# Order of the products inside a step: by part of the weights instead of by k tile

## Chip, cores, metric

The kernel runs on one core of one Trainium2 chip. The metric is device time in microseconds; of several runs the median is given. One more execution was taken with the hardware profiler, and all rows below are from it.

## What is computed

Two layers of a hybrid decoder trunk over 256 tokens of width 2048, all in float32. Each layer normalises its input, projects it with one wide matrix, feeds the columns of the result to four groups of heads (forgetting attention, differential attention, block-sparse attention, gated linear attention), gates each group and projects back:

```python
def reference(x, ...):
    for l in range(DEPTH):                      # DEPTH = 2
        h = rms_norm(x, norm_g[l])              # x: (1, 256, 2048)
        p = split_columns(h @ w_in[l])          # 7,700 columns
        mixed = concatenate([fox, diff, moba, gla])   # four gated head groups
        x = x + mixed @ w_out[l]
    return rms_norm(x, final_norm_g)
```

The large products are `h @ w_in` and `mixed @ w_out`. To keep float32 accuracy with TensorE's faster fp32r type, each operand is split into a high part and a low part, and three products stand for one: high x high, high x low, low x high.

## The kernel before

The weights of both projections are cut into **blocks** of 256 to 512 columns (`_blocks`, line 104), and each block into **steps** of 4 k tiles of 128 rows, or 2 where the block has 512 columns (`_steps`, line 142). The list `plan` holds all steps in the order in which they run. For each step one DMA on the SP queue brings its raw weights (`load`; 4 buffers), ScalarE rounds them to the high part (`hi_of`, line 387), VectorE subtracts to get the low part (`lo_of`, line 390), each into one of 4 buffers (`parts_of`, line 1221), and TensorE multiplies (`multiply`, line 1239). Loads run 4 steps and splits 3 steps ahead of the products.

There are two kinds of blocks that matter here. In a **rows** block the activations are the stationary operand and the weights move: the result has tokens on the partitions, two halves `m` of 128 tokens, each in its own PSUM bank. Per k tile and half there are three matmuls: activations high x weights high, high x low, low x high. All have the block's width: 512, 264 or 258 columns (256 in the last chunk of the output projection). In a **cols** block (256 columns of the weights) the weights are the stationary operand: the result has columns on the partitions, two groups `c` of 128, each in its own bank. Per k tile and group there are two matmuls: the high part with both planes of the activations (`hTp`, high beside low, 512 columns moving), and the low part with the high plane only (256 columns moving). Nine names of 512 columns are cols blocks, each in two halves, in both layers: 144 steps of 4 k tiles x 2 groups, so 8 pairs of matmuls each. A last block (`apart`) and the first step of the plan have orders of their own, which the change leaves alone.

The work of the head groups is written as Python generators (`tasks`). After each step of the plan `give_time` and `tick` let them issue some instructions, by a budget of costs; so small matmuls and transposes into "side" tiles stand on TensorE between steps, never inside one. All matmuls go through the helper `matmul` (line 283 in the rows of the profile), transposes through line 287, and VectorE and ScalarE instructions through line 187, so the profile shows those lines and tells instructions apart by tiles. In the profile a matmul's operands are written `out<-moving,stationary`: `mm<-hTp,hi` is the 512-column matmul of a cols step, `mm<-hTp,lo` the 256-column one; `mm<-hi,hTp`, `mm<-lo,hTp` and, in the output projection, `mm<-hi,mTh`, `mm<-lo,mTh`, `mm<-hi,mTl` are those of rows steps. Block 2 of the plan adds up in a side tile, so its 32 pairs appear as `side<-hTp,hi` and `side<-hTp,lo`.

Every matmul is issued with its own weight load (LDWEIGHTS, engine PEld in the profile).

Of the kernel before, what the change touches and what calls it, by code (L numbers as in the profile page):

```python
# [21 lines left out]
P = 128  # L22
SEQ = 256
# [193 lines left out]
def hybrid_trunk(  # L217
# [63 lines left out]
    def matmul(out, lhsT, rhs, start, stop, tiles=1):  # L281
        left["pe"] += int(np.prod(rhs.shape[1:])) * (4 if lhsT.dtype == F32 else 1) / 2400.0 / tiles
        t_.matmul(out, lhsT, rhs, start=start, stop=stop)  # L283
# [90 lines left out]
    hTp = big.tile([P, KT, 2, SEQ], F32R, name="hTp")  # L374
# [772 lines left out]
    for z in _steps():  # L1147
        b = blocks[z["block"]]
# [90 lines left out]
    def multiply(s):  # L1239
        b = s["block"]  # L1240
        n, (lh, ll) = b["n"], b["lhs"]
        if s["first"]:
            b["ps"] = side.get([P, 1024]) if b is blocks[2] else mm.tile([P, 1024], F32, name="mm")
        ps = b["ps"]
        if b["kind"] == "apart":
            b.setdefault("steps", []).append(s)
            if s["last"]:
                b["ps1"] = side.get([P, 1024])
            for m, o, steps in ((0, ps[:, :n], [s]), (1, b.get("ps1"), b["steps"])):
                if m == 1 and not s["last"]:  # L1250
                    break
                for z in steps:
                    for j, kt in enumerate(z["kts"]):
                        first, last = z["first"] and j == 0, z["last"] and j == len(z["kts"]) - 1
                        hi, lo, ts = z["hi"][:, j], z["lo"][:, j], slice(m * P, (m + 1) * P)
                        matmul(o[:, :n], lh[:, kt, ts], hi, first, False)
                        matmul(o[:, :n], lh[:, kt, ts], lo, False, False)
                        matmul(o[:, :n], ll[:, kt, ts], hi, False, last)
            return
        if s is plan[0]:  # L1260
            for js in ((0, 1), (2, 3)):
                for x, w in ((lh, s["hi"]), (ll, s["hi"]), (lh, s["lo"])):
                    for j in js:
                        for m in range(2):
                            matmul(ps[:, m * 512:m * 512 + n], x[:, j, m * P:(m + 1) * P], w[:, j],
                                   j == 0 and x is lh and w is s["hi"], False)
            return
        for j, kt in enumerate(s["kts"]):
            first, last = s["first"] and j == 0, s["last"] and j == len(s["kts"]) - 1
            hi, lo = s["hi"][:, j], s["lo"][:, j]  # L1270
            if b["kind"] == "rows":
                for m in range(2):
                    o, ts = ps[:, m * 512:m * 512 + n], slice(m * P, (m + 1) * P)
                    matmul(o, lh[:, kt, ts], hi, first, False)
                    matmul(o, lh[:, kt, ts], lo, False, False)
                    matmul(o, ll[:, kt, ts], hi, False, last)
            else:
                for c in range(2):
                    o, cs = ps[:, c * 512:(c + 1) * 512], slice(c * P, (c + 1) * P)
                    matmul(o, hi[:, cs], hTp[:, kt].rearrange("p z t -> p (z t)"), first, False)  # L1280
                    matmul(o[:, :SEQ], lo[:, cs], lh[:, kt], False, last)

    def results(b):
        ps, n = b["ps"], b["n"]
# [44 lines left out]
    for i, s in enumerate(plan):  # L1329
        if ("rb", 0) not in ready:  # L1330
            next(rms, None)
        prepare(i + ahead)
        if i in X_AT:
            c = slice(X_AT.index(i) * 512, X_AT.index(i) * 512 + 512)
            nc.sync.dma_start(xs[:, :, c], x[0, :, c].rearrange("(m p) c -> p m c", p=P))
        settle(waiting, s["first"] and len(waiting) > 1)
        while not s["need"] <= ready:
            tick(False)
        multiply(s)
        if s["last"] and s["block"]["done"]:  # L1340
            waiting.append(s["block"])
        give_time()
        tick()
    while tasks:
        tick(False)
    b = plan[-1]["block"]
# [29 lines left out]
```

## Time and profile before

| | us |
|---|---|
| median of 3 runs | 954.85 (954.78 to 955.5) |
| the profiled execution | 955.05 |
| its span, first to last instruction | 953.3 |
| TensorE matmuls busy | 940.7, 5,430 matmuls |
| TensorE weight loads busy | 819.4, 5,430 loads |
| VectorE busy | 616.8 |
| ScalarE busy | 480.9 |
| GpSimd busy | 68.5 |

The span is what the rows lie in; the profiled execution has 1.75 us more around it. A matmul's duration in the profile runs from its start to the modelled end of its passage through the array. The next one starts before that, so durations overlap and a sum of durations is more than the time they took. The distance between starts is what a matmul costs in a row of matmuls. "Busy" counts overlapping durations once.

### The profile page before, as it was taken

To read this page: it belongs to the slowest core of one execution; us is meant where nothing else is said; L and a number is where in the kernel's file an instruction comes from. 1 tells how busy PE (TensorE), PEld (TensorE's weight loads), DVE (VectorE), ACT (ScalarE), POOL (GpSimd) and SP (SyncE) were. 2 spreads that over 40 slices of the span, in tenths; PEclk is the share of its full clock that TensorE was granted. 3 is DMA by queue.
4 is the path that set the end of the run, shared out by engine and by line. 5 is a ranking of instruction groups with operands and counts; after the bars stand their busy time and mean duration, and the time that the engine had idled before them with its cause. 6 is when DMAs were issued, how large, how long until landed. Compare 5 with 4: busy or idle time off the path is not lost.

```text
span 953.3 us, 13796 instructions
## 1 busy us (share of the span) xinstructions
PE 940.7 (99%) x5430; PEld 819.4 (86%) x5430; DVE 616.8 (65%) x836; ACT 480.9 (50%) x653; POOL 68.5 (7%) x45
## 2 busy tenths in 40 slices
PE   9999999999999999999999999999999999999996
PEld 7989889888888888888898898898888888888886
DVE  7666776667756876555556668656675759755553
ACT  7675534454474446445446544445445644563451
POOL 0010200001110210000000102100011002100000
PEclk9999999999999999999999999999999999999999
DMA  8766565556655465556665544554555645655652
GB/s 312 223 198 204 181 189 157 155 157 195 178 187 178 140 210 163 167 181 180 195 174 161 159 156 155 171 173 156 175 178 177 197 161 177 228 167 165 196 179 89
DMA packets 49075, 170.19 MB, mean 179 GB/s; under 512 B 5969, under 2 KB 6513, under 8 KB 49010
## 3 DMA queue, kind: packets, MB, share of 16 engines
q1 hardware_dynamic: 46592, 165.24, 55.0%
q10 hardware_dynamic: 1778, 1.97, 0.7%
q0 software_dynamic: 640, 2.10, 0.7%
q8 instruction: 42, 0.69, 0.3%
q14 instruction: 23, 0.19, 0.1%
HBM read 167.19 MB, written 2.10 MB: 178 GB/s over the span
## 4 chain that ended last, share of the span: by engine, by line
PE 96%; issue 1%; DVE 1%; ACT 1%; DMA 1%; SPq 0%; POOLq 0%; POOL 0%; DVEq 0%; ACTq 0%
PE mm L283 86%; PE side L283 8%; PE side L287 2%; DMA raw<-in_weights 1%; ACT hi L187 1%; DVE mTl L187 0%; DVE xs L187 0%; DVE lo L187 0%; ACT gate L187 0%; SPq L1158 0%; POOLq L1372 0%; POOL rf L385 0%; ACT two L187 0%; SPq L1171 0%; DVE an L187 0%
## 5 line engine op out<-in xcount | busy, mean ns | idle before, releaser
L187 DVE TENSOR_TENSOR lo<-raw,hi 128x1024 fp32r<-128x1024 f32 (+3 forms) x301 | 380.7, 1269 | 299.7 <-ACT hi L187 296.3
L187 ACT ACTIVATE hi<-raw 128x1024 fp32r<-128x1024 f32 (+3 forms) x301 | 318.1, 1059 | 433.2 <-PE mm L283 390.1
L283 PE MATMUL mm<-hTp,hi 128*128 128x512 f32 x1120 | 397.6, 399 | 0.4 <-ACT gate L187 0.2
L283 PE MATMUL mm<-hTp,lo 128*128 128x256 f32 x1120 | 313.0, 279 | 0.8 <-DVE lo L187 0.8
L283 PE MATMUL mm<-hi,hTp 128*128 128x512 f32 (+2 forms) x1024 | 258.8, 339 | 0.0
L283 PEld LDWEIGHTS mm<-hTp,hi 128*128 128x128 f32 x1120 | 210.3, 188 | 50.2 <-ACT gate L187 0.4
L283 PEld LDWEIGHTS mm<-hTp,lo 128*128 128x128 f32 x1120 | 211.2, 189 | 1.2 <-DVE lo L187 1.1
L283 PEld LDWEIGHTS mm<-hi,hTp 128*128 128x128 f32 x1024 | 176.8, 189 | 21.7 <-ACT hi L187 0.5
L283 PE MATMUL mm<-lo,hTp 128*128 128x512 f32 (+2 forms) x512 | 171.2, 336 | 0.0
L283 PEld LDWEIGHTS mm<-lo,hTp 128*128 128x128 f32 x512 | 96.1, 189 | 9.6
L283 PE MATMUL mm<-hi,mTl 128*128 128x512 f32 (+1 forms) x256 | 96.5, 377 | 0.8 <-DVE mTl L187 0.8
L283 PE MATMUL mm<-hi,mTh 128*128 128x512 f32 (+1 forms) x256 | 96.8, 378 | 0.0
L283 PE MATMUL mm<-lo,mTh 128*128 128x512 f32 (+1 forms) x256 | 96.2, 376 | 0.0
L283 PEld LDWEIGHTS mm<-hi,mTl 128*128 128x128 f32 x256 | 48.2, 188 | 10.4 <-DVE mTl L187 1.7
L283 PEld LDWEIGHTS mm<-lo,mTh 128*128 128x128 f32 x256 | 48.2, 188 | 8.5
L283 PEld LDWEIGHTS mm<-hi,mTh 128*128 128x128 f32 x256 | 48.2, 188 | 8.5
L283 PE MATMUL side<-four,four 128*128 128x128 f32 (+2 forms) x288 | 38.0, 288 | 0.0
L919 POOL TENSOR_TENSOR four<-four,two 128x1024 f32<-128x1024 f32 x8 | 20.8, 2606 | 225.0 <-DVE four L187 225.0
L187 ACT ACT_TABLE_LOAD x27 | 34.6, 1283 | 0.5
L283 PEld LDWEIGHTS side<-four,four 128*128 128x128 f32 (+1 forms) x288 | 31.2, 190 | 2.6 <-issue 0.7
L187 DVE TENSOR_TENSOR both<-mm,both 128x512 f32<-128x512 f32 x35 | 23.9, 684 | 0.0
L187 ACT ACTIVATE four<-side,nb 128x256 f32<-128x256 f32 (+1 forms) x48 | 20.4, 434 | 0.1
(159 smaller groups left out, 618.2 us busy)
## 6 DMA issues: line engine op xcount, KB each, us to landing
raw<-in_weights SPq DMA_DIRECT2D x272, 512.0 KB, 3.7
raw<-in_weights SPq DMA_DIRECT2D x16, 516.0 KB, 3.7
raw<-in_weights SPq DMA_DIRECT2D x15, 528.0 KB, 4.4
xs<-in_x SPq DMA_DIRECT2D x4, 512.0 KB, 4.5
four<-in_xt SPq DMA_DIRECT2D x3, 512.0 KB, 7.1
out<-xs SPq DMA_DIRECT2D x6, 256.0 KB, 3.1
two<-in_const POOLq DMA_DIRECT2D x4, 256.0 KB, 3.6
two<-in_final_norm_g POOLq DMA_DIRECT2D x4, 256.0 KB, 5.6
```

The costliest lines, as they stand in the source:

```text
L187: return f(*args, **kw)
L283: t_.matmul(out, lhsT, rhs, start=start, stop=stop)
L287: t_.transpose(out, src, ident)
L919: g_.tensor_mul(sw, sw, over(f[:, 1], H))
```

## The change

Inside a step, all products with the weights' high part are issued first, then all with the low part. In a cols step that is eight 512-column matmuls and then eight 256-column ones, in place of eight alternating pairs. In a rows step it is high x high for all k tiles and halves, then low x high (both read the weights' high part), then high x low. The matmul that opens a bank's sum is still the first one there, and the one that closes it is now the last product with the low part. Steps, loads, splits, buffers and tasks are as before.

```diff
-        for j, kt in enumerate(s["kts"]):
-            first, last = s["first"] and j == 0, s["last"] and j == len(s["kts"]) - 1
-            hi, lo = s["hi"][:, j], s["lo"][:, j]
-            if b["kind"] == "rows":
-                for m in range(2):
-                    o, ts = ps[:, m * 512:m * 512 + n], slice(m * P, (m + 1) * P)
-                    matmul(o, lh[:, kt, ts], hi, first, False)
-                    matmul(o, lh[:, kt, ts], lo, False, False)
-                    matmul(o, ll[:, kt, ts], hi, False, last)
-            else:
+        order = list(enumerate(s["kts"]))
+        end = s["last"], len(order) - 1
+        if b["kind"] == "rows":
+            for x, part in ((lh, "hi"), (ll, "hi"), (lh, "lo")):
+                for j, kt in order:
+                    for m in range(2):
+                        matmul(ps[:, m * 512:m * 512 + n], x[:, kt, m * P:(m + 1) * P], s[part][:, j],
+                               s["first"] and j == 0 and x is lh and part == "hi", part == "lo" and (True, j) == end)
+            return
+        for part in ("hi", "lo"):
+            for j, kt in order:
                 for c in range(2):
-                    o, cs = ps[:, c * 512:(c + 1) * 512], slice(c * P, (c + 1) * P)
-                    matmul(o, hi[:, cs], hTp[:, kt].rearrange("p z t -> p (z t)"), first, False)
-                    matmul(o[:, :SEQ], lo[:, cs], lh[:, kt], False, last)
+                    o, w = ps[:, c * 512:(c + 1) * 512], s[part][:, j, c * P:(c + 1) * P]
+                    if part == "hi":
+                        matmul(o, w, hTp[:, kt].rearrange("p z t -> p (z t)"), s["first"] and j == 0, False)
+                    else:
+                        matmul(o[:, :SEQ], w, lh[:, kt], False, (True, j) == end)
```

## Rows read from the trace of the kernel before

**Rows 1.** The page: engines (busy, share, instructions), granted clock by slice, chain by engine.

```profile
PE 940.7 (99%) x5430; PEld 819.4 (86%) x5430; DVE 616.8 (65%) x836; ACT 480.9 (50%) x653; POOL 68.5 (7%) x45
...
PEclk9999999999999999999999999999999999999999
...
PE 96%; issue 1%; DVE 1%; ACT 1%; DMA 1%; SPq 0%; POOLq 0%; POOL 0%; DVEq 0%; ACTq 0%
```

**Rows 2.** Groups with shapes apart, whole span: count, busy us, mean ns, idle before.

```profile
L283 PE MATMUL mm<-hTp,hi 128*128 128x512 f32 x1120 | 397.6, 399 | 0.4 <-ACT gate L187 0.2 <-ACT hi L187 0.2
L283 PE MATMUL mm<-hTp,lo 128*128 128x256 f32 x1120 | 313.0, 279 | 0.8 <-DVE lo L187 0.8
...
L283 PE MATMUL mm<-hi,mTl 128*128 128x256 f32 x32 | 9.1, 283 | 0.0
```

**Rows 3.** Timeline, TensorE, 205 to 238 us: start us, duration us, what.

```profile
205.07 0.27 PE L283 MATMUL mm<-hTp,lo 128*128 128x256 f32 x1
...
238.00 0.28 PE L283 MATMUL mm<-hTp,lo 128*128 128x256 f32 x1
```

**Rows 4.** Timeline, TensorE, 326 to 352 us.

```profile
326.99 0.28 PE L283 MATMUL mm<-hTp,lo 128*128 128x256 f32 x1
...
352.08 0.28 PE L283 MATMUL mm<-hTp,lo 128*128 128x256 f32 x1
```

**Rows 5.** Groups with shapes apart, the stretch of rows 3.

```profile
L283 PE MATMUL mm<-hTp,hi 128*128 128x512 f32 x96 | 33.4, 394 | 0.0
L283 PE MATMUL mm<-hTp,lo 128*128 128x256 f32 x96 | 26.6, 277 | 0.0
```

**Rows 6.** Groups with shapes apart, the stretch of rows 4.

```profile
L283 PE MATMUL mm<-hTp,hi 128*128 128x512 f32 x72 | 25.6, 400 | 0.0
L283 PE MATMUL mm<-hTp,lo 128*128 128x256 f32 x72 | 20.2, 281 | 0.0
```

**Rows 7.** Timeline, TensorE, a rows run of 512 columns in the output projection.

```profile
866.08 0.39 PE L283 MATMUL mm<-lo,mTh 128*128 128x512 f32 x1
866.31 0.39 PE L283 MATMUL mm<-hi,mTl 128*128 128x512 f32 x1
866.53 0.39 PE L283 MATMUL mm<-hi,mTh 128*128 128x512 f32 x1
...
872.88 0.39 PE L283 MATMUL mm<-lo,mTh 128*128 128x512 f32 x1
```

**Rows 8.** Timeline, TensorE, where a run of 256 columns follows one of 512.

```profile
922.10 0.39 PE L283 MATMUL mm<-hi,mTl 128*128 128x512 f32 x1
922.33 0.28 PE L283 MATMUL mm<-hi,mTh 128*128 128x256 f32 x1
922.44 0.28 PE L283 MATMUL mm<-lo,mTh 128*128 128x256 f32 x1
922.56 0.28 PE L283 MATMUL mm<-hi,mTl 128*128 128x256 f32 x1
...
923.88 0.28 PE L283 MATMUL mm<-lo,mTh 128*128 128x256 f32 x1
```

**Rows 9.** Timeline, TensorE, where a rows run of 512 columns follows a cols step.

```profile
238.12 0.39 PE L283 MATMUL mm<-hi,hTp 128*128 128x512 f32 x1
...
239.96 0.61 PE L283 MATMUL mm<-hi,hTp 128*128 128x512 f32 x2
```

**Rows 10.** Timeline, TensorE, the first cols step (in brackets: idle before, released by).

```profile
9.53 0.50 PE L283 MATMUL mm<-hTp,hi 128*128 128x512 f32 x1 [0.16 <-ACT hi L187]
10.79 0.39 PE L283 MATMUL mm<-hTp,lo 128*128 128x256 f32 x1 [0.76 <-DVE lo L187]
11.01 0.39 PE L283 MATMUL mm<-hTp,hi 128*128 128x512 f32 x1
```

**Rows 11.** Timeline, the row sums on TensorE and the fold on VectorE before them.

```profile
30.50 0.95 PE L283 MATMUL side<-one,four 128*128 128x1 f32 x8
...
29.22 1.15 DVE L187 TENSOR_TENSOR four<-four 128x512 f32<-128x512 f32 x2
```

**Rows 12.** Waits of ScalarE: who for whom, us in total, times, longest.

```profile
ACT hi L187 <- PE mm L283: 390.1, 222, 6.0
```

## Prediction

> **What bounds the kernel now.** The page comes first, its table of engines and its chain [rows 1]. TensorE is busy for 99% of the span and the chain that ended last is TensorE for 96%, so only what TensorE does per matmul, or what it waits for, can move the time. The granted clock stands at the upper of its two levels, 2.4 GHz, in every slice; the change takes no matmul away, so I leave the clock as it is. Next I ask which matmuls fill the span: the groups of instructions with shapes kept apart [rows 2]. The "cols" blocks give 1,120 pairs of a 512-column matmul (hi) and a 256-column one (lo), and 32 pairs more go to a side tile: 1,152 pairs in 144 steps of 8. The "rows" blocks give runs in which all matmuls have one width. A matmul's duration in these rows is longer than the beat at which matmuls follow each other, because they overlap. So the beats are read from the timeline, as differences of starts.
>
> In one long cols stretch 95 pairs take 32.93 us, 346.6 ns a pair [rows 3]. In another 71 pairs take 25.09 us, 353.4 ns [rows 4]. It is the same code in the same order: the alternation of 512 and 256 has two beats, each held for a whole stretch. Which share has which? The mean duration of a lo matmul is 277 ns in the first stretch and 281 in the second [rows 5, 6], and 279 over the kernel [rows 2], so I take half and half: 350.0 ns a pair.
>
> The runs of one width are steadier. In a settled run of 512-column matmuls 30 of them take 6.80 us, 226.7 ns each [rows 7]; in a run of 256-column matmuls 11 take 1.32 us, 120.0 ns each [rows 8]. Both together are 346.7 ns, the shorter of the two beats.
>
> **The change, part by part.** *The cols steps.* Now: hi, lo, hi, lo. After: eight hi, then eight lo. Nothing is added or removed: as many matmuls, weight loads, bytes. If hi and lo in their groups run at the beats of the settled runs, a pair costs 346.7 ns in place of 350.0, 3.3 ns less. I count 1,104 pairs, the 1,152 less the 48 of the six steps before 30.5 us, which are dealt with below: 1,104 x 3.3 = 3.7 us less.
>
> Two corrections come from the edges of the groups. When a run of 512 follows a lo matmul, its first eight take 1.84 us [rows 9], where eight settled ones take 1.81: some 27 ns to settle. When 256 follows a settled 512 run, the first two take 0.23 us in place of 0.24 [rows 8], some 7 ns won. If each of the 138 steps paid the 27 ns, that would be 3.7 us; if none did, nothing. The settled phase may well carry over from the lo run to the next hi run, as it did from 512 to 256 in two matmuls, and then only steps behind other work of TensorE pay: the two long stretches hold 12 and 9 steps in a row (96 and 72 pairs [rows 5, 6]), so this is a minority, and I take a third, 1.2 us. The 7 ns on 138 steps are 0.9 us. Sum for the cols steps: 3.7 - 1.2 + 0.9 = 3.4 us less; ends 0.9 us less (every step pays) and 4.6 us less (none does). With a share of the long beat of 0.6 instead of a half the upper end is near 5.3.
>
> *The rows steps.* Now for each k tile and half of the rows three matmuls in a row go to one PSUM bank, and the first two have the same stationary tile; after, the bank changes with each matmul. All have one width. The rows show no price for either: from the last matmul of a bank to the first of the other it is 0.22 us, as anywhere in that run [rows 7], and the three of a group share its 0.68 us evenly, so that the one with a repeated stationary tile comes no sooner. I take nothing; TensorE's own back-to-back order covers it, since each weight load lies beside the matmul before it. Each nanosecond of error would be 1.5 us on the 1,536 matmuls of the input projection's rows blocks (16 k tiles x 2 halves x 3 products x 8 blocks x 2 layers), but I see no row that gives the error a sign.
>
> *The first wait.* At 9.53 us TensorE issues one hi matmul and then waits for the low part: its lo starts at 10.79 and the second pair at 11.01 [rows 10], so that the first pair takes 1.48 us where 0.35 would do, 1.13 too much. After the change seven more hi matmuls (1.6 us) lie before the first lo, and the wait goes. What is late next: at 30.50 us TensorE runs the row sums of the first norm, which need a fold on VectorE that ends at 30.37 [rows 11]. That fold hangs on loads of x and on ScalarE and VectorE, which at that time wait for loads and for each other, not for TensorE. So TensorE, come there 1.1 us sooner, would stand still until 30.4, and of the 1.13 us, and of all that the six cols steps before it win, 0.13 is left. Bounds: 0 and 1.1 us; I take 0.1.
>
> *What is moved past what.* Only TensorE's order changes; no DMA and no instruction of VectorE, ScalarE, SP or POOL changes place in its queue. The wait for the low part goes from the second matmul of a step to two thirds of it in rows (after both products with the high part) and to the middle of its matmuls in cols; behind it stand only the lo matmuls of that step. The high part's buffer comes free earlier, by a third of a step, and the low part's at the end as before. ScalarE stands waiting for such buffers for 390 us in 222 places [rows 12], so its next split starts earlier, but TensorE waits for splits only in the place above: worth nothing.
>
> **The sum.** 3.4 + 0.1 = 3.5 us less. The profiled execution is 955.05 us (span 953.3 and 1.75 around it), so 951.55; the median of the three runs is 0.2 lower than it, so the forecast is 951.4.
>
> **Row and rule.** The row: a settled 512 takes 226.7 ns and a settled 256 takes 120.0 [rows 7, 8], 13.3 ns above columns divided by 2.4 GHz, and a pair in alternation has a beat that is not always their sum. [...]
>
> **The rivals.** *(1) Every step pays the settling.* Each hi run is only eight long, as long as the settling, and before it a run of the other width. For it: [rows 9] and the long beat itself show that a change of width upsets the phase. Against it: the 512-to-256 change settles in two. Then the cols steps gain 3.7 - 3.7 + 0.9 = 0.9 us, with the start 1.0: 953.9.
>
> *(2) The order costs nothing.* A matmul's cost is a matter of its own width, and the two beats come from something else in a stretch (other engines' traffic in SBUF, say) that grouping leaves alone. For it: both beats occur in the same code. Against it: the runs of one width keep to one beat through all their stretches. Only the start is left: 954.8. [...]
>
> *(3) Slower: hi keeps its price and lo loses its discount.* In alternation lo is cheap: 279 ns of duration against 283 in a run of its own width [rows 2], so 116 ns of beat in place of 120, and hi takes the rest of the 350, 234. If hi is dear for what it reads (two planes of the activations as the moving operand, against one plane of weights in rows) and not for what stands beside it, then after the change a pair costs 234 + 120 = 354 ns, 4 more: 1,104 x 4 = 4.4 us more, less 0.1: 959.2. The place is every cols step, and it decides from a mean hi beat of 230 ns up. For it: no row shows these operands in a run of 512. Against it: at the short beat a pair with just these operands costs exactly the settled sum.
>
> **How the numbers follow.** A measurement of this kernel can tell about 0.2%, 1.9 us, from no change. Forecast 0.57, rival 1 0.25, rival 2 0.06, rival 3 0.12. The forecast lies beyond 1.9 us but for a small part of its ends: faster 0.56, same 0.32 (rivals 1 and 2 and that part), slower 0.12. The range reaches from the upper end of the gain (5.3 + 0.1: 949.5 against the median) to rival 2 with a little beyond, 955.1; it leaves out rival 3 and the tails, under 2 in 10.
>
> **What would show it.** Right: in cols steps eight hi starts 227 ns apart, then eight lo 120 apart, a step of 2.77 us in place of 2.77 or 2.83; no wait for the low part at 9.5 us, and instead one before the row sums near 30.4. Rival 1: hi starts between 224 and 236 in every step. Rival 3: 234 in the whole hi run. The forecast is wrong if the mean cols step is longer than 2.80 us, if the rows runs leave 227 or 120, or if TensorE shows new waits for splits.

## The result, and the profile after

The median went from 954.85 us to 949.84 (six runs each); the ratio is 0.9946 with a 95% interval of 0.9934 to 0.9959. The profiled execution took 949.76 us, its span 948.0, 5.3 less than before. The forecast of 951.4 lies 1.6 above the result, and the range holds it. But the gain came from another place than the one the forecast rests on.

The groups with shapes kept apart, of the kernel after, answer to [rows 2]:

```profile
L283 PE MATMUL mm<-hTp,hi 128*128 128x512 f32 x1120 | 283.3, 395 | 0.0
L283 PE MATMUL mm<-hTp,lo 128*128 128x256 f32 x1120 | 156.1, 282 | 0.0
```

hi went from 399 to 395 ns and lo from 279 to 282, so a pair won one nanosecond of duration, where the forecast had 3.1 ns of beat (3.4 us over 1,104 pairs). No idle time stands before either any more. The timeline of TensorE, one cols step in the stretch that answers to [rows 3]:

```profile
206.46 2.00 PE L283 MATMUL mm<-hTp,hi 128*128 128x512 f32 x8
208.30 1.11 PE L283 MATMUL mm<-hTp,lo 128*128 128x256 f32 x8
209.25 0.40 PE L283 MATMUL mm<-hTp,hi 128*128 128x512 f32 x1
```

Eight hi take 1.84 us, eight lo 0.95, the step 2.79: 349 ns a pair. This step has no other work before it, and still its hi run is the unsettled one of [rows 9], to the hundredth. The same trace shows it in all 96 steps that follow another cols step directly: their hi runs take 1.840 or 1.841 us.

Now the waits of TensorE (who waits for whom; us in total, times, longest), first of the kernel before:

```profile
PE side L326 <- DVE four L321: 1.3, 1, 1.3
PE side L283 <- DVE mTl L187: 0.9, 1, 0.9
PE mm L283 <- DVE mTl L187: 0.8, 2, 0.4
PE mm L283 <- DVE lo L187: 0.8, 1, 0.8
PE side L287 <- DVE xs L187: 0.4, 2, 0.3
PE side L287 <- DVE an L187: 0.3, 1, 0.3
PE mm L283 <- ACT gate L187: 0.2, 1, 0.2
PE mm L283 <- ACT hi L187: 0.2, 1, 0.2
```

and of the kernel after, where these two are all that is left:

```profile
PE side L326 <- DVE four L321: 1.3, 1, 1.3
PE side L283 <- DVE four L187: 0.7, 1, 0.7
```

The matmuls stand in the same stretches in both kernels, so the length of each stretch, from its first start to the next stretch's first, can be laid side by side. These differ by more than a quarter of a microsecond (the longest cols stretches apart):

| stretch (start in the kernel before) | before | after | change |
|---|---|---|---|
| first two cols blocks' steps, 9.53 us | 6.78 | 5.70 | -1.08 |
| row sums of the first norm, 30.50 | 0.81 | 1.63 | +0.82 |
| cols step and wait before the forget matmuls, 163.04 | 3.85 | 2.88 | -0.97 |
| output projection, layer 0, 394.40 | 19.86 | 19.14 | -0.72 |
| rows step and transposes of layer 1's input, 476.81 | 4.57 | 3.71 | -0.86 |
| transposes of the gate input, 501.84 | 1.04 | 0.25 | -0.79 |
| output projection, layer 1, 864.40 | 57.93 | 57.22 | -0.71 |

The last five sum to 4.05 us: waits that went away. In the list above these waits come to 2.6 us only, because idle time counts from the modelled end of the matmul before: near 403 us it is 0.42, while the next matmul starts 0.81 us after the last one in place of 0.23, and the one behind it 0.34. The beats of the cols steps over the whole kernel give 1.5, the 258-column rows steps lost 0.4, and the start gave 0.3 net. That is the 5.3 of the span within 0.2.

The start went as forecast. After the change the first hi run is not interrupted, and TensorE is at the row sums 1.17 us sooner, where it waits for the fold:

```profile
9.44 2.12 PE L283 MATMUL mm<-hTp,hi 128*128 128x512 f32 x8
...
29.33 0.28 PE L283 MATMUL side<-one,four 128*128 128x1 f32 x2
30.29 0.80 PE L283 MATMUL side<-one,four 128*128 128x1 f32 x6 [0.68 <-DVE four L187]
```

Why did the later waits go? The longest of them, at 166.88 us of the kernel before, is short enough to follow through. Its timeline, TensorE, then ScalarE and VectorE:

```profile
162.92 0.28 PE L283 MATMUL mm<-hi,hTp 128*128 128x258 f32 x1
163.04 0.39 PE L283 MATMUL mm<-hTp,hi 128*128 128x512 f32 x1
...
163.29 1.06 ACT L187 ACTIVATE hi<-raw 128x1024 fp32r<-128x1024 f32 x1 [1.12 <-issue]
...
164.38 1.23 DVE L187 TENSOR_TENSOR lo<-raw,hi 128x1024 fp32r<-128x1024 f32 x1 [2.57 <-ACT hi L187]
165.52 1.22 DVE L187 TENSOR_TENSOR mTl<-side,mTh 128x1024 fp32r<-128x1024 f32 x1
...
166.88 0.47 PE L283 MATMUL side<-four,ones_r 128*128 128x512 f32 x1 [0.87 <-DVE mTl L187]
```

The rows step ends with a matmul that reads the high part (162.92). Just behind its end, at 163.29, ScalarE starts the split that needs its buffer, after 1.12 us in which it did nothing. The profile names no releaser for this split ("issue"); that it waits for the buffer is read from the times here, and tested below by a kernel with one buffer more. VectorE stood still for 2.57 us for the low part; the split of a head group (mTl) has been queued behind it on VectorE, and TensorE's side matmuls wait for that. After:

```profile
159.87 2.18 PE L283 MATMUL mm<-hi,hTp 128*128 128x258 f32 x16
161.89 1.13 PE L283 MATMUL mm<-lo,hTp 128*128 128x258 f32 x8
162.86 0.40 PE L283 MATMUL mm<-hTp,hi 128*128 128x512 f32 x1
...
162.14 1.06 ACT L187 ACTIVATE hi<-raw 128x1024 fp32r<-128x1024 f32 x1 [0.26 <-ACT two L187]
...
163.23 1.23 DVE L187 TENSOR_TENSOR lo<-raw,hi 128x1024 fp32r<-128x1024 f32 x1 [2.60 <-ACT hi L187]
164.37 1.22 DVE L187 TENSOR_TENSOR mTl<-side,mTh 128x1024 fp32r<-128x1024 f32 x1
...
165.74 0.70 PE L283 MATMUL side<-four,ones_r 128*128 128x512 f32 x2
```

All sixteen products with the high part are issued by 161.9. ScalarE starts at 162.14, 1.15 us sooner, where TensorE came only 0.18 sooner, and the whole chain moves with it. ScalarE's waits for TensorE's buffers shrank from 390 us [rows 12] to 366. Most of that is slack, but in the five places of the table work that TensorE needs soon was queued behind it.

### The profile page after: what moved, and what is told of

Same layout as the page of the kernel before. It is cut to its first block, busy times and chain, and to the rows that moved or that the text cites. A ratio compares the mean times of both kernels' runs of the same rounds, so it can differ in the third digit from the quotient of the medians.

```text
span 948.0 us, 13807 instructions
## 1 busy us (share of the span) xinstructions
PE 938.3 (99%) x5430; PEld 822.8 (87%) x5430; DVE 616.6 (65%) x836; ACT 482.0 (51%) x653; POOL 68.3 (7%) x45
## 4 chain that ended last, share of the span: by engine, by line
PE 98%; DVE 1%; issue 1%; POOLq 0%; POOL 0%; ACT 0%; DVEq 0%; ACTq 0%
PE mm L283 87%; PE side L283 8%; PE side L287 2%; PE side L326 0%; DVE lo L187 0%; DVE xs L187 0%; DVE hTp L187 0%; DVE four L187 0%; POOLq L1375 0%; POOL rf L385 0%; ACT two L187 0%; DVEq L1375 0%; DVE four L321 0%; DVE ssf L187 0%; DVE pw L187 0%
## 5 line engine op out<-in xcount | busy, mean ns | idle before, releaser
L283 PE MATMUL mm<-hTp,hi 128*128 128x512 f32 x1120 | 283.3, 395 | 0.0
L283 PE MATMUL mm<-hi,hTp 128*128 128x512 f32 (+2 forms) x1024 | 197.4, 340 | 0.0
L283 PEld LDWEIGHTS mm<-hi,hTp 128*128 128x128 f32 x1024 | 160.0, 189 | 20.9 <-ACT hi L187 0.6
L283 PEld LDWEIGHTS mm<-hTp,lo 128*128 128x128 f32 x1120 | 152.8, 190 | 11.1
L283 PE MATMUL mm<-hTp,lo 128*128 128x256 f32 x1120 | 156.1, 282 | 0.0
L283 PE MATMUL mm<-lo,hTp 128*128 128x512 f32 (+2 forms) x512 | 104.8, 336 | 0.0
L283 PEld LDWEIGHTS mm<-lo,hTp 128*128 128x128 f32 x512 | 81.3, 188 | 10.0
L283 PE MATMUL mm<-hi,mTh 128*128 128x512 f32 (+1 forms) x256 | 65.1, 378 | 0.0
L283 PE MATMUL mm<-hi,mTl 128*128 128x512 f32 (+1 forms) x256 | 64.4, 376 | 0.0
L283 PE MATMUL mm<-lo,mTh 128*128 128x512 f32 (+1 forms) x256 | 64.4, 376 | 0.0
```

## The experiments

I had three theories. **A**: the high part's buffer comes free a third of a step earlier, and with it everything queued behind the next split on ScalarE and VectorE. **B**: all of the gain is the beat of the matmuls. **C**: the waits near 403 and 873 us go because the new order needs the low plane of the activations later in its step. Each ratio is to the kernel before, run on the same chip; its median there was 955.12 us for the first three kernels and the last one, 954.71 for the three with raw buffers as they were, and 955.11 for the four after those.

**Cols steps alone in the new order.**

```diff
         if b["kind"] == "rows":
-            for x, part in ((lh, "hi"), (ll, "hi"), (lh, "lo")):
...
+            for j, kt in enumerate(s["kts"]):
...
+                for m in range(2):
...
+                    matmul(o, lh[:, kt, ts], hi, first, False)
+                    matmul(o, lh[:, kt, ts], lo, False, False)
+                    matmul(o, ll[:, kt, ts], hi, False, last)
```

> Cols steps in the new order, rows steps in the old. Theory A (the high part's buffer comes free a third of a step earlier, so ScalarE's split, and what stands behind it on ScalarE and VectorE, comes earlier, and TensorE's few waits for these shrink): the beats give 1.5 us, the start 0.4, and the waits that lie behind cols steps go, near 165 us (1.0) and near 502 (0.8), while those in and behind rows steps, near 403, 480 and 873 us, stay (2.3): 954.85 - 3.7 = 951.2. Theory B (all of the gain is the beat of the matmuls, and waits come and go by chance): the cols beats carry it, 950 to 950.5.

Measured: 952.54 us, ratio 0.9975 (0.9966 to 0.9985). Its waits of TensorE:

```profile
...
PE side L283 <- DVE mTl L187: 0.9, 1, 0.9
PE mm L283 <- DVE mTl L187: 0.8, 2, 0.4
PE side L287 <- DVE xs L187: 0.4, 2, 0.3
PE side L283 <- DVE four L187: 0.3, 1, 0.3
```

B fails by 2 us. Of the waits only those at the gate input (502 us) went, and the first one. The wait near 165 us stayed, against A's number; the rows above say why: the split there waits for the buffer of a rows step, and I had put it behind the cols step that TensorE happens to be in. With that 1.0 us moved A says 952.2. The beats of its cols steps give 1.4 us in the trace.

**Rows steps alone in the new order** (the same edit the other way round).

> Rows steps in the new order, cols steps in the old. Theory A: the waits near 403, 480 and 873 us go (2.3 us), the runs of 258 columns lose 0.4, and the beats of cols and the waits near 165 and 502 stay: 953.0. Theory B: rows have one width, nothing to gain: 954.9 to 955.3.

Measured: 950.27 us, ratio 0.9952 (0.9939 to 0.9964), nearly all of the gain, though the beat of its rows runs won nothing. Its waits:

```profile
...
PE mm L283 <- ACT hi L187: 0.8, 1, 0.8
PE mm L283 <- DVE lo L187: 0.8, 1, 0.8
PE side L287 <- DVE an L187: 0.3, 1, 0.3
PE mm L283 <- ACT gate L187: 0.2, 1, 0.2
```

The waits for mTl and xs are gone. After the start just those are left that the kernel before has behind cols steps, at 502 us (an, gate). The other two are at the start: the low part's, as before, and one for a high part at 8.5 us, which loads of x that landed later in this execution brought in (0.7 us). So each wait goes with the kind of step that holds the buffer. The rest of its gain neither theory expected: 2.3 us from cols steps whose code is untouched. They alternate as before, but long stretches that had the long beat have the short one. Timeline, the stretch that answers to [rows 4]:

```profile
326.38 0.27 PE L283 MATMUL mm<-hTp,lo 128*128 128x256 f32 x1
...
350.65 0.27 PE L283 MATMUL mm<-hTp,lo 128*128 128x256 f32 x1
```

70 pairs in 24.27 us, 346.7 ns, where it was 353.4. What decides which of its beats an alternating stretch falls into is not settled by these runs. But the 1.5 us of cols beats in the kernel after can't be put down to grouping alone: with the rows steps in the new order, cols steps that alternate win 2.3 us, and grouped ones 1.5. What grouping adds to this kernel is the first wait and the one at 502 us, and its median of 949.84 against 950.27 is no clear difference.

**Grouped, but one product with the high part held back to the end of each step.**

```diff
+        todo = [("hi", j, kt, c) for j, kt in order for c in range(2)]
+        todo = todo[:-1] + [("lo", j, kt, c) for j, kt in order for c in range(2)] + todo[-1:]
...
```

(in rows steps the last product of low activations and high weights in the same way)

> The new order, but one product with the high part is held back to the end of each step, so that this buffer comes free as late as before; in rows the products with the activations' low part stay as late as in the new order but for that one. Theory A: the waits come back (3 to 4 us of 4.0 after the start) and the beats stay: 953 to 954. Theory B: the runs of one width are as long as before but for one matmul, so about the time of the new order, 949.8 to 950.5. Theory C (the waits near 403 and 873 us went because the new order needs the low activations later in a step): those two stay away and the others come back, 952.

Measured: 953.73 us, ratio 0.9988 (0.9979 to 0.9997). One matmul's place in each step takes away most of the gain:

```profile
...
PE side L283 <- DVE four L187: 0.9, 1, 0.9
PE side L283 <- DVE mTl L187: 0.9, 1, 0.9
PE side L287 <- DVE xs L187: 0.4, 2, 0.3
PE side L287 <- DVE an L187: 0.4, 1, 0.4
PE mm L283 <- ACT gate L187: 0.2, 1, 0.2
```

Three of the five waits are back in full, as A says. The two of the large matmuls for mTl are not in this list: the output projection of layer 0 takes 19.40 us here, against 19.86 before and 19.14 after. So C holds for these two: needing the low activations later hides most of a wait that the late buffer brings back (0.46 of 0.72 us). The kernels with a fifth buffer below show that the buffer alone is enough there too, so in these two places the change has two causes.

**The old order with a fifth buffer for the high part.** This is A without any change of TensorE's order. It needs room, so one of the four raw buffers goes; a control has three raw buffers and nothing else.

```diff
-RAW_BUFS = 4
+RAW_BUFS = 3
...
-            t = wst.tile([P, PART_W], F32R, name=name, bufs=PART_BUFS)
+            t = wst.tile([P, PART_W], F32R, name=name, bufs=PART_BUFS + (name == "hi"))
```

> The old order with three buffers for raw weights in place of four (a control for the next kernel, which needs the room): loads land in 3.7 us and a step takes 2.8, so all theories expect about the time of before, 954.9, or some tenths more at the start.

> The old order, three raw buffers, and five buffers for the high part: a split of ScalarE then waits for the step before last, not for the last one, and never stands in the way. Theory A: the waits near 165, 403, 480, 502 and 873 us go without any change of TensorE's order, 4.0 us below the control, some 951. Theory B: TensorE's order is as before, so the time of the control.

> The new order, three raw buffers and five buffers for the high part. Theory A: TensorE has no wait left after the start for the earlier split to take away, so 949.5 to 950. Theory B: as after, 949.8.

Measured: the control 965.22 us (1.0114, 1.0097 to 1.0132), the old order with five 961.76 (1.0072, 1.0057 to 1.0087), the new order with five 965.12 (1.0103, 1.0086 to 1.0119). The control missed by 10 us, so the three are not clean. Two things had come in. With three raw buffers the start is later: the row sums at 30.5 us take 1.85, 2.42 and 4.48 us of TensorE's time in the three, against 0.81 before. And every long run of 512 columns had become slower, 7.2 us in all in the control. One of its groups, first in the kernel before, then in the control:

```profile
L283 PE MATMUL mm<-hi,mTh 128*128 128x512 f32 x224 | 87.8, 392 | 0.0
```

```profile
L283 PE MATMUL mm<-hi,mTh 128*128 128x512 f32 x224 | 89.0, 397 | 0.0
```

After the start the two kernels with five buffers have no wait of TensorE left but one of 0.6 us behind "issue" in the new order.

Dropping a raw buffer of 4,224 bytes moves the split buffers, the moving operand of these matmuls, by an odd multiple of 128 bytes (33 x 128); the activations stay where they were. The next four kernels put this apart. The first two have the raw buffers as wide as the split ones (4,352 bytes), so that the split buffers are moved by a multiple of 256 bytes (3 x 4,352 in place of 4 x 4,224). These places follow from the widths in the code; no trace shows addresses.

```diff
-        raw = wst.tile([P, STEP_W], F32, name="raw", bufs=RAW_BUFS)
+        raw = wst.tile([P, PART_W], F32, name="raw", bufs=RAW_BUFS)
```

> The old order, three raw buffers again, but each as wide as a split buffer, so that the split buffers lie 128 bytes from a multiple of 256, as in the kernel before; in the first control they lay on multiples of 256. If the place of the moving operand is what took the settled 512-column beat from 227 to 232 ns there, it is 227 again and the 7.2 us of the rows runs are back: 955 to 958, the rest being the later loads of the start. If the missing buffer itself did it: 965.

> The same with five buffers for the high part, TensorE's order as before. Theory A: the waits near 165, 403, 480, 502 and 873 us are gone, 4 us below this control in the stretch after the start. Theory B: the time of the control.

Measured: control 958.59 us (1.0037, 1.0025 to 1.0050), with five buffers 954.37 (0.9990, 0.9980 to 0.9999), 4.2 us less in the same TensorE order. The rows runs of 512 columns are back at the length of before in the control (330.96 us in sum, before 330.92). The waits of the two kernels, control first:

```profile
...
PE side L283 <- DVE mTl L187: 0.9, 1, 0.9
PE mm L283 <- DVE mTl L187: 0.8, 2, 0.4
...
PE side L287 <- DVE xs L187: 0.4, 2, 0.3
PE side L287 <- DVE an L187: 0.3, 1, 0.3
PE mm L283 <- ACT gate L187: 0.2, 1, 0.2
```

```profile
PE side L283 <- DVE four L187: 2.1, 1, 2.1
PE side L326 <- DVE four L321: 1.3, 1, 1.3
PE mm L283 <- DVE lo L187: 0.9, 2, 0.8
PE mm L283 <- DVE hTp L187: 0.5, 1, 0.5
```

Everything after the start is gone, and the stretches, against the control, show the sizes of the change itself: 1.03 us near 165, 0.73 and 0.72 in the output projections, 0.86 at layer 1's input, 0.90 at the gate input. They sum to 4.2 us. That is theory A, shown by another edit.

The other two test the place alone, in the kernel before: 128 unused bytes ahead of the raw and split buffers, or ahead of the activations as well.

```diff
+    pad = wst.tile([P, 32], F32, name="pad", bufs=1)
+    nc.vector.memset(pad, 0.0)
```

(in the second kernel from the pool `cp`, which lies ahead of the activations)

> The kernel before with 128 bytes of unused memory ahead of the raw and split buffers, nothing else. If place sets the beat: the rows runs of 512 columns go to 232 ns, some 7 us, 961 to 963. If not: 954.9.

> The kernel before with the same 128 bytes ahead of the activations too, so that both operands of a large matmul move together. If the beat hangs on where the operands lie to each other: 954.9. If it hangs on the place of the moving operand alone: 961 to 963 or, where cols runs change too, further off.

Measured: 962.77 us (1.0081, 1.0066 to 1.0096) with the split buffers moved, 954.51 (0.9996, 0.9986 to 1.0005) with both moved. In the first the runs of 512 columns have the durations of the first control, here the same group:

```profile
L283 PE MATMUL mm<-hi,mTh 128*128 128x512 f32 x224 | 89.0, 397 | 0.0
```

and in the second those of the kernel before (392 ns). So the slower beat does not come from where the split buffers lie by themselves: with the activations moved as well it is gone. The activations moved alone, which would make the rule whole, were not run.

The place of the operands sets the beats of the alternating cols steps too. With the split buffers moved, the stretch that answers to [rows 4] reads:

```profile
328.83 0.28 PE L283 MATMUL mm<-hTp,lo 128*128 128x256 f32 x1
...
353.75 0.28 PE L283 MATMUL mm<-hTp,lo 128*128 128x256 f32 x1
```

71 pairs in 24.92 us are 351 ns. In the kernel before, the 19 stretches of three steps or more have 346.6 to 346.7 ns or 353.2 to 353.4, and nothing between; here all 19 have 350.0 to 351.1. With both moved the two beats are back, but the stretch at 308.8 us has the short one, where the kernel before had the long one: TensorE's order need not change for that.

**Every second cols step with the low part first**, so that half of the changes from 256 to 512 columns go away.

```diff
-        for part in ("hi", "lo"):
+        flip = s["kts"][0] // 4 % 2 == 1
+        for part in (("lo", "hi") if flip else ("hi", "lo")):
...
```

(the matmul that closes a bank's sum is then the last one with the high part)

> As the new order, but every second cols step takes its products with the low part first, so that half of the changes from 256 to 512 columns, each of which costs some 27 ns to settle, go away: 70 x 20 ns (27 less 7) = 1.4 us less by beats, 948.4. By theory A the high part's buffer comes free at the end of those steps, so up to half of the 1.8 us of waits behind cols steps comes back: 948.4 to 949.8. By theory B: 948.4.

Measured: 948.77 us, ratio 0.9938 (0.9924 to 0.9951), the fastest of all; its interval overlaps that of the kernel after, so that it beats it is likely and not shown. In the trace it does what it should: cols steps take 0.9 us less in all than after, where 1.4 was expected, and the waits near 165, 403, 480, 502 and 873 us stay away.

## Why the prediction was right, and where it was not

**The cols steps** were mis-sized: forecast 3.4 us less, measured 1.5. The step that failed is the share of the settling, "this is a minority, and I take a third". Each hi run pays it, also in the middle of long stretches; the mechanism was rival 1's, and so was its sign: the hi starts of those 96 steps lie 226 to 236 ns apart. The other two terms held: eight unsettled hi 1.84 us, and the two-matmul step from 512 to 256 (0.23 us). Rival 1's sum was 0.9. The 68 steps inside a stretch won 5.6 ns each, 0.4 us, which is its size (6.5 ns); the other 71, at the ends of stretches, won 1.1 without the wait at 166.9 us. Why those won more stays open, and the kernel with the rows steps alone shows that cols beats move without any change of cols steps. (There are 139 steps behind the row sums, not 138: five lie before them, not six.)

**The rows steps** were right for the 512-column runs, whose length in all did not change (0.00 us in the input projection). The 258-column ones, priced at nothing, ran 0.4 us longer in the new order, 1.1 ns for each of 384 matmuls; why stays open.

**The first wait** was right in kind: it moved to the row sums. In place of 0.13 us 0.3 was left, since the fold ended at 30.15 in place of 30.37.

**The buffer that comes free earlier** was where the prediction failed most. "TensorE waits for splits only in the place above: worth nothing" was priced at 0 and measured 4.05 us (in two of the five places, near 403 and 873 us, the later need of the low activations would have won most of it too). I had looked for waits of TensorE for a split. The five waits bear other names (mTl, xs, an, gate), because what TensorE waits for there is work queued behind a split on VectorE or ScalarE. The sum came near since one term was 1.9 too high and the other 4.05 too low. That the result lies in the range is luck: the range reached down to 949.5 for a larger share of the long beat, and not for any wait. Of its own signs of being wrong two came up, in a small size: all 139 cols steps, counted to the next start of TensorE, have a mean of 2.817 us (2.835 before), over its 2.80, though those inside stretches take 2.793, and the 258-column runs went from some 120 to 122 ns.

**Rivals 2 and 3**: the beats did change, though by less than a nanosecond and a half a pair, and hi did not keep its 234 ns: eight take 1.84 us, 230 each, just where rival 3 turns, but the last four of the eight start 227 to 231 ns apart, where rival 3 had 234 in the whole run. Rival 1's mechanism was there, but its time of 953.9 was not: it too had the earlier buffer at nothing. The Trainium skill ("TensorE: Matmul & The Clock Gate", section "Back-to-back issue gap") gives N / 2.4 + 2.5 ns at the upper clock for an isolated matmul of N columns, and about 131 ns a matmul at 512 columns for a stream of weight loads and matmuls. The trace agrees with neither figure: here each matmul has its own weight load, and one of 512 columns costs 227 ns, or a mean of 230 in the first eight behind another width.

## What to carry to other kernels

A buffer's late release is passed on to all that is queued behind the instruction that waits for it: near 165 us here the split came 1.15 us sooner, and the work of VectorE behind it and the matmul that waited for that came 1.15 and 1.14 sooner. So when an edit moves the last reader of a buffer, look at what stands behind the refilling instruction on its engine, and whether the bound engine ever waits for that, under any name. The last reader's place, or one more buffer, can be tried apart from the order, as here: one more buffer won the same 4 us, and one last reader put back cost 3.4 of the 5.3 us of the span.

## What the runs showed that I had not expected

The settled beat of a 512-column fp32r matmul with its own weight load hangs on where its operands lie in SBUF to each other, as far as these runs go: 227 ns as in the kernel before or with both moved by 128 bytes, some 232 with the moving operand alone moved by that, 7.2 us over 1,440 matmuls. A tile of 128 bytes, or one buffer fewer elsewhere, is enough, so an experiment that changes a buffer count needs a control for place. And an alternation of 512 and 256 columns can hold either of two beats, 346.7 or 353.4 ns a pair, for a whole stretch, in unchanged code: rows steps in another order changed the beat of some stretches, all operands moved by 128 bytes that of one, and the split buffers moved alone gave 351 in all.
